# Rotary embedding on one core: the opening store of zeros and batch 0's one-row store are taken out, and the five loads are issued first

## The chip, the cores and the metric

The kernel runs on one core of a Trainium2 chip. The metric is the device time of one execution in microseconds (us). The kernel before took 316.7 us as the median of three runs (316.62 to 316.84). A core has five engines that work side by side, each on its own list of instructions: VectorE (DVE in the profile), ScalarE (ACT), GpSimd (POOL), SyncE (SP) and TensorE, which has no work here. Data between the chip's main memory (HBM) and the core's own memory of 128 partitions moves by DMA. A DMA is issued by an engine and carried out by 16 DMA engines, which serve several queues: here the one that GpSimd fills (q0 in the profile) and the one that SyncE fills (q1).

## The reference

The input `x` has 8 batches of 2048 positions, 16 heads and 64 values each, in float32: 8.39 MB a batch. Each head is rotated by the angles of its position:

```python
def reference(x, cos, sin):                      # cos, sin: 2048 x 32
    x1 = x[..., :head_dim // 2]
    x2 = x[..., head_dim // 2:]
    cos = cos[None, :, None, :]
    sin = sin[None, :, None, :]
    out1 = x1 * cos - x2 * sin
    out2 = x1 * sin + x2 * cos
    return np.concatenate([out1, out2], axis=-1).astype(np.float32)
```

So the whole input is read once and the whole output is written once, with two products and a sum for each value.

## The kernel before, in words

A batch is one tile `xt` of 128 partitions: partition p holds positions 16p to 16p + 15, which the code calls its `J` = 16 rows, of 1024 values each. "One row" below means one of these sixteen on all partitions. The tile is float16 while HBM holds float32, so a load and a store convert on the way; both are issued by GpSimd. There are `NBUF` = 5 tiles, so batches 5, 6 and 7 are loaded into the tiles of batches 0, 1 and 2, and each of these loads waits until the store of that earlier batch has landed.

*Constants.* SyncE issues three loads: `sin` (L40), `head`, which is the first two rows of batch 0 in float32 (L41), and `cos` (L45). ScalarE converts them to float16: `sin_h` with a negated half (L95, L96), the two rows into batch 0's tile (L91), and `cos_h` (L97).

*Rotation.* `rotate` is three VectorE operations on whole rows: the product with `sin_h` into a temporary tile `v` (L73), the product with `cos_h` in place (L79), and the sum (L81). Batch 0 is rotated in two parts: rows 0 and 1, which came by `head`, and then the 14 rows that load 0 brings. The other batches are rotated whole.

*Order on GpSimd's queue.* The code writes out the start of it as `ring`: load 0, the opening store, load 1, the one-row store `first`, then loads 2, 3 and 4. The opening store (L85) writes one float32 zero into the first value of each partition's first row of batch 0's output: 128 values in all. `first` (L107) writes row 0 of batch 0, waits for its rotation, and also waits for the opening store to have landed, since it overwrites the zeros. Then `store` (L60) writes batch 0 from row 1 on (15 rows). The order of the later stores and loads is chosen when the kernel is built, by the planner of the framework, from the waits that each has; GpSimd then takes its instructions in that fixed order, and an instruction that waits holds up all behind it. In the profile the order after load 4 is: stores of batches 0 and 1, loads 5 and 6, stores 2 and 3, load 7, stores 4, 5 and 6.

*The end.* Batch 7 leaves in three parts: rows 0 to 8 (`gate`, L141), rows 9 to 13 (`rest`, L143), and rows 14 and 15, which ScalarE converts back to float32 (L151) and SyncE stores (L152) once `gate` has landed.

Of the kernel before, what the change touches and what calls it, by code (L numbers as in the profile page):

```python
# [1 line left out]

# [4 lines left out]


@with_exitstack  # L10
def kernel(
    ctx: ExitStack,
    tc: tile.TileContext,
    x: bass.AP,
    cos: bass.AP,
    sin: bass.AP,
    out: bass.AP,
):
    nc = tc.nc
    f16 = mybir.dt.float16  # L20
    f32 = mybir.dt.float32

    B, S, H, D = x.shape
    Dh = D // 2
    P = nc.NUM_PARTITIONS
    J = S // P
    NBUF = 5

    const_pool = ctx.enter_context(tc.tile_pool(name="rope_const", bufs=1))
    io_pool = ctx.enter_context(tc.tile_pool(name="rope_io", bufs=NBUF))  # L30
    tmp_pool = ctx.enter_context(tc.tile_pool(name="rope_tmp", bufs=1))

    JA = 2
    head = const_pool.tile([P, JA, H, D], f32)
    x0 = x[0].rearrange("(p j) h d -> p j (h d)", j=J)
    sin_f = const_pool.tile([P, J, Dh], f32)
    cos_f = const_pool.tile([P, J, Dh], f32)
    cos_h = const_pool.tile([P, J, Dh], f16)
    sin_h = const_pool.tile([P, J, D], f16)
    nc.sync.dma_start(out=sin_f, in_=sin.rearrange("(p j) d -> p j d", j=J))  # L40
    nc.sync.dma_start(  # L41
        out=head.rearrange("p j h d -> p (j h d)"),
        in_=x0[:, 0:JA, :].rearrange("p j f -> p (j f)"),
    )
    nc.sync.dma_start(out=cos_f, in_=cos.rearrange("(p j) d -> p j d", j=J))  # L45

    loads = []

    def load(b):
        xt = io_pool.tile([P, J, H, D], f16)  # L50
        j0 = JA if b == 0 else 0
        dma = nc.gpsimd.dma_start(  # L52
            out=xt[:, j0:J, :, :].rearrange("p j h d -> p (j h d)"),
            in_=x[b].rearrange("(p j) h d -> p j (h d)", j=J)[:, j0:J, :].rearrange("p j f -> p (j f)"),
        )
        loads.append(dma)
        return xt

    def store(b, xt, j0=0):
        return nc.gpsimd.dma_start(  # L60
            out=out[b].rearrange("(p j) h d -> p j (h d)", j=J)[:, j0:J, :].rearrange("p j f -> p (j f)"),
            in_=xt[:, j0:J, :, :].rearrange("p j h d -> p (j h d)"),
        )

    def rotate(xt, j0, j1):
        v = tmp_pool.tile([P, J, H, D], f16)
        n = j1 - j0
        js = slice(j0, j1)
        shape = [P, n, H, 2, Dh]
        sin_b = sin_h[:, js, :].rearrange("p j (e d) -> p j e d", e=2).unsqueeze(2).to_broadcast(shape)  # L70
        cos_b = cos_h[:, js, :].unsqueeze(2).to_broadcast([P, n, 2 * H, Dh])
        xe = xt[:, js, :, :].rearrange("p j h (e d) -> p j h e d", e=2)
        nc.vector.tensor_mul(  # L73
            out=v[:, js, :, :].rearrange("p j h (e d) -> p j h e d", e=2),
            in0=xe[:, :, :, ::-1, :],
            in1=sin_b,
        )
        xw = xt[:, js, :, :].rearrange("p j h (e d) -> p j (h e) d", d=Dh)
        nc.vector.tensor_mul(out=xw, in0=xw, in1=cos_b)  # L79
        xa = xt[:, js, :, :].rearrange("p j h d -> p (j h d)")  # L80
        nc.vector.tensor_add(out=xa, in0=xa, in1=v[:, js, :, :].rearrange("p j h d -> p (j h d)"))  # L81


    tiles = [load(0)]
    opening = nc.gpsimd.dma_start(  # L85
        out=out[0].rearrange("(p j) h d -> p j (h d)", j=J)[0:P, 0, 0:1],
        in_=nc.const_aps.tensor(0.0, [P, 1], f32),
        allow_slow_non_contiguous=True,
    )
    tiles.append(load(1))  # L90
    nc.scalar.copy(  # L91
        out=tiles[0][:, 0:JA, :, :].rearrange("p j h d -> p (j h d)"),
        in_=head.rearrange("p j h d -> p (j h d)"),
    )
    nc.scalar.copy(out=sin_h[:, :, Dh:D], in_=sin_f)  # L95
    nc.scalar.mul(out=sin_h[:, :, 0:Dh], in_=sin_f, mul=-1.0)  # L96
    nc.scalar.copy(out=cos_h, in_=cos_f)  # L97
    rotate(tiles[0], 0, JA)
    def part(b, j0, j1):
        return (  # L100
            out[b].rearrange("(p j) h d -> p j (h d)", j=J)[:, j0:j1, :].rearrange("p j f -> p (j f)"),
            tiles[b][:, j0:j1, :, :].rearrange("p j h d -> p (j h d)"),
        )

    def store_rows(b, j0, j1):
        dst, src = part(b, j0, j1)
        return nc.gpsimd.dma_start(out=dst, in_=src)  # L107

    first = store_rows(0, 0, 1)
    tc.add_manual_dep(  # L110
        first.ins,
        opening.ins.name,
        mybir.DependencyInfo(mybir.DependencyClass.Sync, mybir.DependencyReason.DATA),
        reason="the result replaces the zeros",
    )
    ring = [loads[0], opening, loads[1], first]
    for b in range(2, NBUF):
        tiles.append(load(b))
        ring.append(loads[b])
    for a, b in zip(ring[1:], ring[:-1]):  # L120
        tc.add_manual_dep(
            a.ins,
            b.ins.name,
            mybir.DependencyInfo(mybir.DependencyClass.NoSync, mybir.DependencyReason.DATA),
            reason="order of the ring",
        )
    for b in range(B):
        rotate(tiles[b], JA if b == 0 else 0, J)
        if b < B - 1:
            st = store(b, tiles[b], 1 if b == 0 else 0)  # L130
            if b == 0:
                tc.add_manual_dep(
                    st.ins,
                    first.ins.name,
                    mybir.DependencyInfo(mybir.DependencyClass.NoSync, mybir.DependencyReason.DATA),
                    reason="order of the ring",
                )
        if b + NBUF < B:
            tiles.append(load(b + NBUF))
    dst, src = part(B - 1, 0, 9)  # L140
    gate = nc.gpsimd.dma_start(out=dst, in_=src)  # L141
    dst, src = part(B - 1, 9, J - JA)
    rest = nc.gpsimd.dma_start(out=dst, in_=src)  # L143
    tc.add_manual_dep(
        rest.ins,
        gate.ins.name,
        mybir.DependencyInfo(mybir.DependencyClass.NoSync, mybir.DependencyReason.DATA),
        reason="order of the ring",
    )
    dst, src = part(B - 1, J - JA, J)  # L150
    nc.scalar.copy(out=head.rearrange("p j h d -> p (j h d)"), in_=src)  # L151
    end = nc.sync.dma_start(out=dst, in_=head.rearrange("p j h d -> p (j h d)"))  # L152
    tc.add_manual_dep(
        end.ins,
        gate.ins.name,
        mybir.DependencyInfo(mybir.DependencyClass.Sync, mybir.DependencyReason.DATA),
        reason="the last rows go out behind this part",
    )


# [1 line left out]
_INS = ['x', 'cos', 'sin']  # L162
_OUTS = [((8, 2048, 16, 64), 'float32')]


# [23 lines left out]
```

## Time and profile before

| What | Value |
|---|---|
| Median of three runs | 316.7 us (316.62 to 316.84) |
| Span of the profiled execution | 314.8 us |
| VectorE busy | 209.1 us (66% of the span), 27 instructions |
| ScalarE busy | 6.8 us (2%), 6 instructions |
| GpSimd busy | 10.4 us (3%), 23 instructions |
| VectorE, one whole batch, each of three operations | 8.692 us |
| GpSimd, one DMA issue | 0.53 to 0.67 us |
| VectorE's idle time that loads of x ended | 29.8 us, in two waits (4.84 and 24.96) |

The median lies 1.9 us above the profiled span: the span runs from the first to the last instruction of one profiled execution.

The trace gives for each DMA the time of its issue and the time from issue to landing. Their sum is the time at which it landed:

| DMA | Issued, us | To landing, us | Landed, us |
|---|---|---|---|
| load 0 (14 rows) | 1.25 | 22.2 | 23.45 |
| cos | 1.63 | 22.0 | 23.63 |
| opening store | 1.92 | 21.9 | 23.82 |
| load 1 | 2.45 | 40.9 | 43.35 |
| `first` (1 row) | 27.13 | 17.5 | 44.63 |
| load 2 | 27.65 | 36.3 | 63.95 |
| load 4 | 28.71 | 73.8 | 102.51 |
| store 0 (15 rows) | 50.11 | 70.6 | 120.71 |
| store 1 | 76.29 | 63.8 | 140.09 |
| load 5 | 121.29 | 38.0 | 159.29 |
| load 6 | 140.34 | 38.3 | 178.64 |
| store 2 | 140.86 | 57.1 | 197.96 |
| load 7 | 198.29 | 38.3 | 236.59 |
| store 4 | 198.82 | 57.1 | 255.92 |
| store 6 | 211.99 | 82.6 | 294.59 |
| `gate` (9 rows) | 263.09 | 42.4 | 305.49 |
| `rest` (5 rows) | 263.62 | 47.9 | 311.52 |
| rows 14 and 15, by SyncE | 305.55 | 8.4 | 313.95 |

How to read it: a DMA that is issued early waits in the queue behind the earlier ones, so the time to landing is mostly waiting. The difference of two neighbours' landings is the time that the later one had the DMA engines for. The trace also has a record of every packet that a DMA engine moved, with its start, length and size; a whole batch is 128 packets, one for each partition, eight on each of the 16 engines.

### The profile page before, as it was taken

To read this page: it belongs to the slowest core of one execution; us is meant where nothing else is said; L and a number is where in the kernel's file an instruction comes from. 1 tells how busy PE (TensorE), PEld (TensorE's weight loads), DVE (VectorE), ACT (ScalarE), POOL (GpSimd) and SP (SyncE) were. 2 spreads that over 40 slices of the span, in tenths; PEclk is the share of its full clock that TensorE was granted. 3 is DMA by queue.
4 is the path that set the end of the run, shared out by engine and by line. 5 is a ranking of instruction groups with operands and counts; after the bars stand their busy time and mean duration, and the time that the engine had idled before them with its cause. 6 is when DMAs were issued, how large, how long until landed. Compare 5 with 4: busy or idle time off the path is not lost.

```text
span 314.8 us, 125 instructions
## 1 busy us (share of the span) xinstructions
DVE 209.1 (66%) x27; ACT 6.8 (2%) x6; POOL 10.4 (3%) x23
## 2 busy tenths in 40 slices
DVE  0108999999999999999679999980009993000000
ACT  3200000000000000000000000000000002000000
POOL 2002000000000000010000000200000001000000
DMA  9899999999999899999999999999999999999998
GB/s 283 187 262 200 200 266 200 200 262 204 200 200 325 375 500 400 400 333 266 200 200 212 387 400 400 475 458 266 200 300 433 400 400 525 408 400 400 433 427 339
DMA packets 3201, 101.71 MB, mean 323 GB/s; under 512 B 385, under 2 KB 385, under 8 KB 769
## 3 DMA queue, kind: packets, MB, share of 16 engines
q0 software_dynamic: 2624, 99.09, 98.1%
q1 hardware_dynamic: 576, 2.62, 2.2%
q14 instruction: 1, 0.00, 0.0%
HBM read 67.63 MB, written 67.11 MB: 428 GB/s over the span
## 4 chain that ended last, share of the span: by engine, by line
DVE 25%; another core or an unknown queue 20%; DMA 19%; issue 18%; ACT 1%; POOL 1%; SPq 0%; POOLq 0%; DVEq 0%; ACTq 0%
DMA xt<-in_x_dram 12%; DVE xt L81 8%; DVE xt L79 8%; DVE v L73 8%; DMA cos_f<-in_cos_dram 7%; ACT head L151 1%; POOL out_dram L60 0%; POOL xt L52 0%; ACT cos_h L97 0%; SPq L41 0%; SPq L40 0%; POOLq L52 0%; DVEq L73 0%; ACTq L151 0%
## 5 line engine op out<-in xcount | busy, mean ns | idle before, releaser
L73 DVE TENSOR_TENSOR v<-xt,sin_h 128x16384 f16<-128x16384 f16 (+2 forms) x9 | 69.7, 7744 | 40.0 <-DMA xt<-in_x_dram 29.8
L79 DVE TENSOR_TENSOR xt<-xt,cos_h 128x16384 f16<-128x16384 f16 (+2 forms) x9 | 69.7, 7744 | 13.4 <-ACT cos_h L97 13.1
L81 DVE TENSOR_TENSOR xt<-xt,v 128x16384 f16<-128x16384 f16 (+2 forms) x9 | 69.7, 7744 | 0.3
L52 POOL DMA_DIRECT2D xt<-in_x_dram x8 | 4.4, 557 | 120.2 <-DMA out_dram<-xt 119.4
L151 ACT CAST head<-xt 128x2048 f32<-128x2048 f16 x1 | 1.9, 1897 | 238.6 <-DVE xt L81 238.6
L60 POOL DMA_DIRECT2D out_dram<-xt x7 | 3.7, 535 | 58.6 <-DVE xt L81 58.6
L141 POOL DMA_DIRECT2D out_dram<-xt x1 | 0.5, 533 | 50.6 <-DVE xt L81 50.6
L91 ACT CAST xt<-head 128x2048 f16<-128x2048 f32 x1 | 1.9, 1897 | 3.4 <-DMA head<-in_x_dram 3.4
L107 POOL DMA_DIRECT2D out_dram<-xt x1 | 0.5, 531 | 24.1 <-DVE xt L81 24.1
L95 ACT ACT_TABLE_LOAD x1 | 1.3, 1283 | 0.7 <-PEq L173 0.7
L97 ACT CAST cos_h<-cos_f 128x512 f16<-128x512 f32 x1 | 0.6, 617 | 13.7 <-DMA cos_f<-in_cos_dram 13.7
L95 ACT CAST sin_h<-sin_f 128x512 f16<-128x512 f32 x1 | 0.6, 617 | 1.5 <-DMA sin_f<-in_sin_dram 1.5
L96 ACT ACTIVATE sin_h<-sin_f 128x512 f16<-128x512 f32 x1 | 0.6, 624 | 0.0
L85 POOL DMA_DIRECT2D out_dram<-const-float32-0.0 x1 | 0.5, 545 | 0.0
L143 POOL DMA_DIRECT2D out_dram<-xt x1 | 0.5, 533 | 0.0
L173 POOL MEMSET const-float32-0.0<- 128x1 f32 x1 | 0.1, 98 | 0.2 <-issue 0.2
L173 POOL MEMSET const-bfloat16-1.0<- 128x1 bf16 x1 | 0.1, 101 | 0.0
L173 POOL MEMSET const-float32-1.0<- 128x1 f32 x1 | 0.1, 98 | 0.0
L173 POOL MEMSET const-uint8-127<- 128x1 uint8 x1 | 0.1, 98 | 0.0
## 6 DMA issues: line engine op xcount, KB each, us to landing
xt<-in_x_dram POOLq DMA_DIRECT2D x7, 4096.0 KB, 38.3
out_dram<-xt POOLq DMA_DIRECT2D x1, 7680.0 KB, 70.6
out_dram<-xt POOLq DMA_DIRECT2D x1, 4608.0 KB, 42.4
xt<-in_x_dram POOLq DMA_DIRECT2D x1, 3584.0 KB, 22.2
out_dram<-xt POOLq DMA_DIRECT2D x1, 2560.0 KB, 47.9
head<-in_x_dram SPq DMA_DIRECT2D x1, 1024.0 KB, 6.9
out_dram<-head SPq DMA_DIRECT2D x1, 1024.0 KB, 8.4
out_dram<-xt POOLq DMA_DIRECT2D x1, 512.0 KB, 17.5
```

What stands on the lines that cost most here:

```text
L52: dma = nc.gpsimd.dma_start(out=xt[:, j0:J, :, :].rearrange("p j h d -> p (j h d)"), in_=x[b].rearrange("(p j) h d -> p j (h d)", j=J)[:, ...
L60: return nc.gpsimd.dma_start(out=out[b].rearrange("(p j) h d -> p j (h d)", j=J)[:, j0:J, :].rearrange("p j f -> p (j f)"), in_=xt[:, j0:J ...
L73: nc.vector.tensor_mul(out=v[:, js, :, :].rearrange("p j h (e d) -> p j h e d", e=2), in0=xe[:, :, :, ::-1, :], in1=sin_b,)
L79: nc.vector.tensor_mul(out=xw, in0=xw, in1=cos_b)
L81: nc.vector.tensor_add(out=xa, in0=xa, in1=v[:, js, :, :].rearrange("p j h d -> p (j h d)"))
L85: opening = nc.gpsimd.dma_start(out=out[0].rearrange("(p j) h d -> p j (h d)", j=J)[0:P, 0, 0:1], in_=nc.const_aps.tensor(0.0, [P, 1], f32 ...
L91: nc.scalar.copy(out=tiles[0][:, 0:JA, :, :].rearrange("p j h d -> p (j h d)"), in_=head.rearrange("p j h d -> p (j h d)"),)
L95: nc.scalar.copy(out=sin_h[:, :, Dh:D], in_=sin_f)
L96: nc.scalar.mul(out=sin_h[:, :, 0:Dh], in_=sin_f, mul=-1.0)
L97: nc.scalar.copy(out=cos_h, in_=cos_f)
L107: return nc.gpsimd.dma_start(out=dst, in_=src)
L151: nc.scalar.copy(out=head.rearrange("p j h d -> p (j h d)"), in_=src)
```

## The change

The opening store goes, with its place in `ring` and the dependency of `first` on it. `first` goes with its helper `store_rows`, and batch 0's store writes all 16 rows. `ring` then holds the five loads alone, so GpSimd issues them without a store between them.

```diff
     tiles = [load(0)]
-    opening = nc.gpsimd.dma_start(
-        out=out[0].rearrange("(p j) h d -> p j (h d)", j=J)[0:P, 0, 0:1],
-        in_=nc.const_aps.tensor(0.0, [P, 1], f32),
-        allow_slow_non_contiguous=True,
-    )
     tiles.append(load(1))
...
-    def store_rows(b, j0, j1):
-        dst, src = part(b, j0, j1)
-        return nc.gpsimd.dma_start(out=dst, in_=src)
-
-    first = store_rows(0, 0, 1)
-    tc.add_manual_dep(
-        first.ins,
-        opening.ins.name,
-        mybir.DependencyInfo(mybir.DependencyClass.Sync, mybir.DependencyReason.DATA),
-        reason="the result replaces the zeros",
-    )
-    ring = [loads[0], opening, loads[1], first]
+    ring = [loads[0], loads[1]]
     for b in range(2, NBUF):
...
         if b < B - 1:
-            st = store(b, tiles[b], 1 if b == 0 else 0)
-            if b == 0:
-                tc.add_manual_dep(
-                    st.ins,
-                    first.ins.name,
-                    mybir.DependencyInfo(mybir.DependencyClass.NoSync, mybir.DependencyReason.DATA),
-                    reason="order of the ring",
-                )
+            store(b, tiles[b])
```

## The prediction

> **What bounds the kernel now.** I read the page's slices and queues first, because a kernel that moves eight batches in and out and does three vector operations on each can only be bound by one of these two.
>
> ```profile
> DVE  0108999999999999999679999980009993000000
> ...
> DMA  9899999999999899999999999999999999999998
> ...
> q0 software_dynamic: 2624, 99.09, 98.1%
> q1 hardware_dynamic: 576, 2.62, 2.2%
> ...
> HBM read 67.63 MB, written 67.11 MB: 428 GB/s over the span
> ```
>
> The vector engine (DVE) has holes; the DMA row has none. GpSimd's queue (q0) and SyncE's (q1) together fill the 16 DMA engines for 98.1% + 2.2% of the span. So the end is set by how much time the transfers need, plus any moment in which the engines have nothing queued. Next I read the timeline of GpSimd (POOL), which says when each transfer enters the queue, with the two places where DVE waits for data.
>
> ```profile
> 1.25 0.67 POOL L52 DMA_DIRECT2D xt<-in_x_dram  x1 [0.81 <-PEq L184]
> ...
> 1.92 0.55 POOL L85 DMA_DIRECT2D out_dram<-const-float32-0.0  x1
> 2.45 0.54 POOL L52 DMA_DIRECT2D xt<-in_x_dram  x1
> ...
> 27.13 0.53 POOL L107 DMA_DIRECT2D out_dram<-xt  x1 [24.14 <-DVE xt L81]
> 27.65 1.60 POOL L52 DMA_DIRECT2D xt<-in_x_dram  x3
> ...
> 50.11 0.54 POOL L60 DMA_DIRECT2D out_dram<-xt  x1 [20.85 <-DVE xt L81]
> ...
> 76.29 0.54 POOL L60 DMA_DIRECT2D out_dram<-xt  x1 [25.64 <-DVE xt L81]
> ...
> 121.29 0.53 POOL L52 DMA_DIRECT2D xt<-in_x_dram  x1 [44.47 <-DMA out_dram<-xt]
> ...
> 140.34 0.53 POOL L52 DMA_DIRECT2D xt<-in_x_dram  x1 [18.51 <-DMA out_dram<-xt]
> 140.86 1.06 POOL L60 DMA_DIRECT2D out_dram<-xt  x2
> ...
> 159.38 8.69 DVE L73 TENSOR_TENSOR v<-xt,sin_h 128x16384 f16<-128x16384 f16 x1 [4.84 <-DMA xt<-in_x_dram]
> ...
> 198.29 0.53 POOL L52 DMA_DIRECT2D xt<-in_x_dram  x1 [56.37 <-DMA out_dram<-xt]
> ```
>
> Columns: start in us, length, engine, line, operation, and in brackets the idle time before it with what ended it. With each transfer's time to landing (the table of landings above) this gives the queue's order: transfers land in the order in which they were issued, one behind the other. From the landing of batch 0's store (120.71) to that of batch 6's (294.59) nine whole batches pass: 173.88 / 9 = **19.32 us for a batch**, a load and a store alike. A transfer is always issued long before its turn: batch 0's store enters at 50.11, while loads are due until 102.51. Issue times therefore have slack of tens of us, and only what the queue carries counts.
>
> **What the change removes, part by part.**
>
> *The opening store* (128 values of 4 bytes, one for each partition). Its issue, 0.55 us on POOL, is in front of load 1 only, which then enters at 1.92 instead of 2.45; load 0 is moving until 23.45, which hides that. In the queue it is an item between load 0 and load 1. It landed 0.37 us behind load 0 (23.82 against 23.45); part of that is the way of its completion, as the packet records give its data 15 ns on each engine. Cost between 0 and 0.37; I take 0.05, since the 15 ns are its own row.
>
> *The one-row store* `first`. One row of sixteen is worth 19.32 / 16 = 1.21 us by the rate. It landed 44.63 - 43.35 = 1.28 behind load 1. There is a third row: from load 0's landing to load 2's, 63.95 - 23.45 = 40.50 us pass, and two loads are worth 38.64, so 1.86 us go to all that is small there: opening, `first`, the last packet of `cos` (it rides between load 0 and load 1), and something more. The packet records show the something: the last packet of load 1 took 2.70 to 2.89 us on fifteen of the 16 engines, where such a packet takes 2.43 everywhere else. It is the packet ahead of `first`. So `first` costs between 1.28 and 1.86; by the records 1.24 (spacing of the packets) + 0.33 (the slowed packet) = 1.57, which I take.
>
> *Batch 0's store* grows from 15 rows to 16: 120.71 - 102.51 = 18.20 now, 19.32 then: +1.12.
>
> *Issues.* POOL loses two of them, 0.55 + 0.53 us, and the wait of 24.14 us for the first rotation; loads 2 to 4 go in at about 2.5 to 4.1 us instead of 27.65 to 29.25. Nothing waits for them sooner: load 1 keeps the engines until 43. The number of transfers in the queue at once becomes five at the start; in the trace five whole ones stand there too, from 211.99 (batch 3's store, load 7, batches 4, 5 and 6), and the issue then took 0.53 as ever. So I cost the early issue at nothing; if the queue did hold POOL up, it would do so with a full queue, and behind it on POOL stands only batch 0's store, which has about 50 us of cover.
>
> *The wait that lengthens: `cos`.*
>
> ```profile
> 1.63 22.05 DMA cos_f<-in_cos_dram
> ...
> 23.70 0.63 ACT cos_h L97
> ```
>
> This is the chain of waits near the start. `cos` (256 KB on SyncE's queue) needs 22 us because its packets take turns with load 0's, one against one; its completion is a packet of its own, which now gets its turn while the opening's tiny packet stands on the other side. Without the opening, load 1's first packet stands there: 19.32 / 8 = 2.42 us (a batch is 128 rows, eight for each engine). I expect `cos` to land at about 26.1 instead of 23.7 and with it DVE's first products and every DVE operation up to batch 4 to be 2.4 us late. What is late next: batch 0's store is issued at about 52.5, with its turn at about 101, so 48 us of cover; batch 1's at 78.7, turn at about 120. The delay ends at batch 5, where DVE waits 4.84 us for load 5 anyway and would then wait 2.4. Cost on the end: nothing.
>
> **The sum**: -0.05 (opening) - 1.57 (`first`) + 1.12 (the sixteenth row) = -0.50 us. From both sides: -0 - 1.28 + 1.12 = -0.16 and, all small things together, -1.86 + 1.12 = -0.74. The slowed packet need not vanish: if it belongs to the first change from loading to storing, it moves to load 4, and the saving is 0.50 - 0.33 = 0.17. Between these I take 0.4, nearer to the records. The profiled execution's span goes from 314.8 to 314.4. The median of the runs is 1.9 above that span, which lies around it and isn't touched: 316.7 - 0.4 = **316.3 us**.
>
> The Trainium skill speaks of each transfer's fixed cost (DMA: Bandwidth & Descriptors, Anatomy of one DMA): about 2.0 us on top of the bytes. By that the two transfers removed would be worth 4.0 us. The row against it: the last but one store (five rows) landed 6.0 us behind the nine rows ahead of it, and 5/16 of 19.32 is 6.04, so behind a full queue no fixed cost shows.
>
> **The rivals.**
> - *Each transfer costs its setup.* Speaking for it: the 1.86 us above, more than the bytes of one row. Against: the five-row store, and 19.32 for nine batches in a row, each a transfer. Its size from rows: a load on an empty queue, load 0, lands 22.2 us after issue; its 14 rows are 16.9 and sin, cos and head (1.5 MB at that rate) 3.6, so 1.7 us of setup; two of them are 3.4: 316.7 - 3.4 - 0.2 = 313.1. The skill's figure would give 312.5.
> - *Nothing is saved*: the slowed packet goes with the first real store wherever it stands, and the extra 0.58 between the landings of loads 0 and 1 (19.90 for a load) is `cos`. Then 0.1 to 0.2 remain: 316.6.
> - *A dry queue (slower).* POOL takes its instructions in a written order, which the build's planner chooses; now it is stores 0 and 1, loads 5 and 6, stores 2 and 3, load 7, stores 4 to 6. With two instructions fewer ahead, the planner could put load 5 ahead of store 1. Load 5 waits for store 0 to land; store 1, ready at 76, would be stuck behind it, and at 120.7 the engines would stand still. Price: 0.55 from landing to the load's issue, plus 1.7 of setup as for load 0 (2.2 by sin: 2.8 to landing, 0.6 of it bytes), so 2.3 to 2.8 each. In that order it happens at stores 0, 1 and 2, so about 7.5 us: 323.8. It decides as soon as one load of the second round precedes a store that could cover it. Against it: store 1 is ready 44 us before store 0 lands, and that isn't close. A flip the other way (store 2 ahead of load 5) costs nothing, as the queue stays full.
> - *`cos` reaches the end (slower).* 2.4 us late all the way: 316.3 + 2.4 = 318.7. It decides from a delay of 4.84 us, at batch 5; even then the last store is issued at 263.09 for a turn at 294.59. Against it, then, both margins.
>
> **How the numbers follow.** Forecast 0.65, setup 0.03, nothing saved 0.14, dry queue 0.12, `cos` to the end 0.06. What a measurement of this kernel can tell from no change is about 0.2%, 0.63 us. The forecast's own range, 0.16 to 0.74 saved and 0.2 for the spread of runs (316.62 to 316.84), is 315.8 to 316.7; a third of its chance lies beyond 0.63 saved. Faster: 0.03 + 0.22 = 0.25. Slower: 0.12 + 0.06 = 0.18. Same: 0.57. For the range I leave out setup, the dry queue and the far half of the `cos` case: 315.6 to 317.4.
>
> **What would show it.** In the profile after: five loads issued by about 4.1 us; `cos` landing at about 26 us and DVE's second operation at about 26.8; the landings of loads 1 to 4 19.3 apart, load 2 landing at about 62.3; store 0 landing 19.3 behind load 4, at about 120.3; DVE's wait before batch 5 down from 4.84 to about 2; the end of everything 0.4 earlier; POOL's order as now. A packet of 2.7 us or more ahead of store 0 would show that the slowing belongs to the first store. I'd be wrong if the DMA row had a hole, if load 5 were issued before store 1, or if a batch took other than 19.3 us while loads follow loads.

## The result and the profile after

The changed kernel takes 317.3 us (median of 20 runs, 316.99 to 317.63) against 316.67 for the kernel before (20 runs beside it): a ratio of 1.002, 95% interval 1.0015 to 1.0026. It is slower by 0.63 us, 0.2% of the time, where 0.4 us faster was forecast. The profiled span went from 314.8 to 315.5 us.

The page of the changed kernel, its queues and HBM:

```profile
span 315.5 us, 121 instructions
...
DMA  9899999999999999999999999999999999999998
...
q0 software_dynamic: 2448, 99.09, 98.0%
q1 hardware_dynamic: 576, 2.62, 2.2%
HBM read 67.63 MB, written 67.11 MB: 427 GB/s over the span
```

The bytes are the same and the DMA row still has no hole at this resolution, so the lost time isn't a queue that ran dry. Its timeline (start, length, engine, line, operation, idle time before with what ended it):

```profile
1.25 2.79 POOL L52 DMA_DIRECT2D xt<-in_x_dram  x5 [0.80 <-PEq L161]
...
54.94 0.54 POOL L60 DMA_DIRECT2D out_dram<-xt  x1 [50.91 <-DVE xt L81]
...
81.12 0.54 POOL L60 DMA_DIRECT2D out_dram<-xt  x1 [25.64 <-DVE xt L81]
...
121.72 0.53 POOL L52 DMA_DIRECT2D xt<-in_x_dram  x1 [40.06 <-DMA out_dram<-xt]
...
141.31 0.53 POOL L52 DMA_DIRECT2D xt<-in_x_dram  x1 [19.06 <-DMA out_dram<-xt]
141.83 1.06 POOL L60 DMA_DIRECT2D out_dram<-xt  x2
...
160.09 8.69 DVE L73 TENSOR_TENSOR v<-xt,sin_h 128x16384 f16<-128x16384 f16 x1 [0.72 <-DMA xt<-in_x_dram]
```

The five loads go in at once and the order on GpSimd is the same as before. The answers for the DMAs issued at 2.95 (load 3), 3.47 (load 4) and 54.94 (store 0), with the time to landing as the last number, say where the loss arises:

```profile
xt<-in_x_dram POOLq DMA_DIRECT2D x1, 4096.0 KB, 78.7
...
xt<-in_x_dram POOLq DMA_DIRECT2D x1, 4096.0 KB, 98.6
...
out_dram<-xt POOLq DMA_DIRECT2D x1, 66.5
```

They landed at 81.7, 102.1 and 121.4. In the kernel before, loads 3 and 4 were issued at 28.18 and 28.70:

```profile
xt<-in_x_dram POOLq DMA_DIRECT2D x1, 4096.0 KB, 55.0
...
xt<-in_x_dram POOLq DMA_DIRECT2D x1, 4096.0 KB, 73.8
```

So there load 4 landed 19.3 us behind load 3. Store 0's landing is now 0.7 us later than the 120.7 of before, which is the whole loss. Load 4 had the engines for 20.4 us and store 0 for 19.3; a batch takes 19.32. The packet records name the place: on all 16 engines the last packet of load 4, the one ahead of the first store, took 3.1 to 3.7 us instead of 2.43, on the mean **1.03 us** too long. In the kernel before, the same happened at the last packet of load 1, ahead of `first`, with 0.35 us. No later change from loading to storing shows it, in either kernel.

By the starts of the packets, from load 1 to store 1: the new slow packets cost +1.03, the old ones are gone, -0.35, and 16 rows in place of `first` and 15 rows give -0.04. That is +0.64 of the 0.72 us between the spans.

### The profile page after: what moved, and what is told of

Its sections match the earlier page's. It is cut to its first block, busy times and chain, and to the rows that moved or that the text cites. A ratio compares the mean times of both kernels' runs of the same rounds, so it can differ in the third digit from the quotient of the medians.

```text
span 315.5 us, 121 instructions
## 1 busy us (share of the span) xinstructions
DVE 209.1 (66%) x27; ACT 6.8 (2%) x6; POOL 9.3 (3%) x21
## 4 chain that ended last, share of the span: by engine, by line
DVE 25%; DMA 21%; another core or an unknown queue 18%; issue 18%; POOL 1%; ACT 1%; SPq 0%; POOLq 0%; DVEq 0%; ACTq 0%
DMA xt<-in_x_dram 12%; DMA cos_f<-in_cos_dram 9%; DVE xt L81 8%; DVE xt L79 8%; DVE v L73 8%; ACT head L128 1%; POOL out_dram L60 1%; POOL xt L52 0%; ACT cos_h L92 0%; SPq L41 0%; SPq L40 0%; POOLq L60 0%; DVEq L73 0%; ACTq L128 0%
```

## The experiments

The question is why the slow packets cost 0.35 us ahead of the one-row store and 1.03 ahead of the whole one. Each timed experiment has its ratio against the kernel before, run on the same chip. "Slow packets" are the us by which the packets of a transfer are longer than usual, as a mean over the 16 engines, each with the transfer in which they stand. They come from the packet records of one profiled execution of each kernel. The medians are over 8 to 20 executions, except where it says one run, and over three for the kernel before:

```
kernel                       early              in load 4    median us
before                       0.35 (load 1)      0            316.7
after                        0                  1.03         317.3
no opening                   0.33 (load 1)      0            316.68
no one-row store             0                  1.38         317.48
opening into batch 7         0                  0.79         317.34
opening on SyncE             0                  1.02         317.43
one row behind load 4        0                  0.64         317.44
store 0 behind load 2        1.28 (load 2)      0            317.55
two rows behind load 1       1.03 (load 1)      0            317.37
one head behind load 1       0                  1.18         317.28
half a row behind load 1     0.05 (load 1)      0.65         316.79
copy inside the core         1.23 (load 1)      0            319.93, one run
copy from HBM to HBM         0                  0.98         319.62, one run
rows by SyncE's queue        0.22 (load 1)      0.24         320.42, one run
two halves together, once    0.63 (load 2)      1.16         316.92
two halves together, again   0.26 (load 1)      0            316.82
two halves apart             0.03 (load 1)      0.18         316.43
three halves apart           0.07 (load 1)      0            316.50
```

The slow packets reach the end nearly one for one. Add up all that is too long in the packets of the first five loads, and the time of the same profiled execution goes with the sum: 0.2 to 0.3 us of it and 316.4 to 316.5 us (two and three halves apart), 0.35 to 0.4 and 316.6 (before, no opening, two halves again), 0.74 and 316.92 (half a row), 1.1 to 1.5 and 317.2 to 317.7 (the eight others that move the same bytes). The first execution of the two halves together alone stands outside, at 1.96 and 318.92.

**The opening store alone left out.**

```diff
-    opening = nc.gpsimd.dma_start(...)
...
-    ring = [loads[0], opening, loads[1], first]
+    ring = [loads[0], loads[1], first]
```

> The opening store alone is left out; the one-row store and the order of the loads stay. The result showed that the last packets ahead of the first real store of the queue are slow: 0.33 us over the usual 2.43 in the kernel before, 1.01 us over it in the changed kernel. Theory A (the opening pays beforehand what the first store costs): the slow packets ahead of the one-row store grow from about 0.33 to about 1.0 us over, and the time is about 0.6 us above before, like the changed kernel's 317.3. Theory B (the cost goes by the size of the first real store, or by what is queued ahead of it, and the opening does nothing but let cos land earlier): the slow packets stay at 0.33 us over, and the time is within 0.1 us of before.

Ratio 0.9997 (0.9988 to 1.0006), slow packets 0.33: theory A fails. No effect of the opening on the time can be seen (the interval is -0.4 to +0.2 us). What it did was to let `cos` land early: ScalarE's conversion, which waits for it, starts at 28.29 here and at 23.70 with the opening.

**The one-row store alone left out.**

```diff
-    first = store_rows(0, 0, 1)
...
-    ring = [loads[0], opening, loads[1], first]
+    ring = [loads[0], opening, loads[1]]
...
-            st = store(b, tiles[b], 1 if b == 0 else 0)
+            store(b, tiles[b])
```

> The opening store stays, the one-row store alone is left out, so that batch 0 leaves as one store and the five loads go first with the opening between loads 0 and 1. Theory A (the opening pays beforehand): the last packets of load 4 are at most 0.33 us over 2.43, the time is 0.3 to 0.5 us below before (about 316.2). Theory B (size of the first store, or what is queued ahead of it): the last packets of load 4 are about 1.0 us over, and the time is 0.6 us above before.

Ratio 1.0026 (1.0016 to 1.0035), slow packets 1.38 in load 4. The whole loss of the change comes with this part of it.

**An opening elsewhere, and on another queue.**

The first diff is against the changed kernel, the second against the first:

```diff
     tiles = [load(0)]
+    opening = nc.gpsimd.dma_start(
+        out=out[B - 1].rearrange("(p j) h d -> p j (h d)", j=J)[0:P, 0, 0:1],
+        in_=nc.const_aps.tensor(0.0, [P, 1], f32),
...
-    ring = [loads[0], loads[1]]
+    ring = [loads[0], opening, loads[1]]
```

```diff
-    opening = nc.gpsimd.dma_start(
-        out=out[B - 1].rearrange("(p j) h d -> p j (h d)", j=J)[0:P, 0, 0:1],
+    opening = nc.sync.dma_start(
+        out=out[0].rearrange("(p j) h d -> p j (h d)", j=J)[0:P, 0, 0:1],
...
-    ring = [loads[0], opening, loads[1]]
+    ring = [loads[0], loads[1]]
```

> The changed kernel with an opening store again, but into the first values of batch 7's output instead of batch 0's. If the cost belongs to the addresses that are written first (the opening must touch the same part of the output), the last packets of load 4 stay 1.0 us over and the time stays 0.6 above before. If it belongs to the queue or to the DMA engines (any store opens them), they are at most 0.33 over and the time is 0.3 to 0.5 below before.

> The changed kernel with the opening store again, to batch 0's output, but issued by SyncE on its own queue behind cos. If the cost belongs to GpSimd's queue, the last packets of load 4 stay 1.0 us over and the time is 0.6 above before. If it belongs to the DMA engines or to the addresses, they are at most 0.33 over and the time is 0.2 to 0.5 below before.

Ratios 1.0020 (1.0010 to 1.0029) and 1.0026 (1.0015 to 1.0036); load 4 is slow by 0.79 and 1.02. A store of 4 bytes a partition takes nothing off the cost that these runs could show, wherever it goes. The 0.79 came with about 0.4 us of slightly long packets spread over loads 1 to 4 of that execution.

**Size or place?** The one-row store moved behind load 4 (against the kernel without the opening):

```diff
-    first = store_rows(0, 0, 1)
-    ring = [loads[0], loads[1], first]
+    ring = [loads[0], loads[1]]
     for b in range(2, NBUF):
         tiles.append(load(b))
         ring.append(loads[b])
+    first = store_rows(0, 0, 1)
+    ring.append(first)
```

And the whole store moved ahead of load 3 (against the changed kernel):

```diff
+    rotate(tiles[0], JA, J)
     for b in range(2, NBUF):
+        if b == 3:
+            ring.append(store(0, tiles[0]))
         tiles.append(load(b))
...
```

The later loop then leaves batch 0 out.

> Five loads first, no opening, and then the one-row store, now behind load 4, with the other 15 rows behind it. So far: the opening changes nothing (without it the slow packets ahead of the one-row store were 0.34 us over the usual 2.43; with it and without the one-row store, those of load 4 were 1.35 over). Theory B1 (the cost of the first large transfer out goes by the size of its packets: 4 KB for one row, 64 KB for a whole batch): the last packets of load 4 are about 0.3 over, nothing more between the one-row store and the 15 rows, and the time is that of before (316.6 to 316.8). Theory B2 (it goes by what is ahead: five loads in a row instead of two): they are about 1.0 over, and the time is 317.3 to 317.6.

> No opening and no one-row store; batch 0 leaves as one store, but ahead of loads 3 and 4 instead of behind them. Theory B1 (size of the packets): the last packets of load 2, ahead of that store, are 1.0 to 1.4 us over 2.43, as those of load 4 are in the changed kernel; time 317.3 to 317.5. Theory B2 (number of loads ahead): with three loads ahead they are about 0.5 over (between the 0.33 for two and the 1.0 to 1.3 for five); time about 316.9. Under both, the queue is never empty, although the order of the later loads and stores differs from the changed kernel.

The whole store costs 1.28 with three loads ahead as with five (ratio 1.0031, 1.0011 to 1.0051), so the number of loads ahead isn't it. The one row right ahead of the other 15 costs 0.64, between the two theories, and the time is that of the changed kernel (ratio 1.0023, 1.0011 to 1.0035). The profiled execution also had 0.57 us of long packets within loads 2 and 3, which bring the sum to 1.28; why they are there stays open.

**The early store's size.** Two rows, one head (64 values) and half a row instead of one row, behind load 1, with no opening. `row0` and `src0` are batch 0's output and tile with all 16 rows of a partition in one line; the later store of batch 0 begins where the early one ends. In this order:

```diff
-    first = store_rows(0, 0, 1)
+    first = store_rows(0, 0, JA)
```

```diff
-    first = store_rows(0, 0, 1)
+    first = nc.gpsimd.dma_start(out=row0[:, 0:D], in_=src0[:, 0:D])
```

```diff
-    first = store_rows(0, 0, 1)
+    first = nc.gpsimd.dma_start(out=row0[:, 0:8 * D], in_=src0[:, 0:8 * D])
```

> The early store behind load 1 takes two rows (packets of 8 KB) instead of one, batch 0's other store 14; no opening. Theory B1 (size): the last packets of load 1 are over by a little more than with one row, 0.35 to 0.45 us. Theory B2 (what is ahead): 0.28 to 0.34, as with one row. Time within 0.2 us of before under both.

> The early store behind load 1 takes one head of row 0 alone (64 values, packets of 256 bytes out), the other store of batch 0 everything else; no opening. Theory B1 (size): the last packets of load 1 are less than 0.3 us over, near 0, and either the first large store (behind load 4) then pays 1.0 after all, as it did behind the opening store of 4 bytes (time 317.4), or nothing is left to pay and the time is 0.2 to 0.3 below before. Theory B2: as with one row, 0.3 over, nothing behind load 4, time as before.

> The early store behind load 1 takes half of row 0 (8 heads, packets of 2 KB out), the other store of batch 0 everything else; no opening. So far, over the usual 2.43 us: packets of 256 bytes cost nothing early and left 1.18 behind load 4; 4 KB cost 0.33 early and left nothing; 8 KB cost 1.03 early and left nothing. Theory B1 (size): about 0.15 to 0.2 early, nothing behind load 4, time 0.1 to 0.2 us below before. Rival (there is a least size that settles it, between 256 bytes and 4 KB): nothing or little early, and 1.0 to 1.4 behind load 4, time 317.3.

Two rows pay the full 1.03 early and leave nothing (ratio 1.0014, 1.0004 to 1.0025); neither expectation had more than 0.45 there. One head pays nothing and leaves 1.18 (1.0014, 1.0005 to 1.0023). Half a row came out as neither of its two expectations, and is the telling one: it pays 0.05 and takes part of the rest away, 0.65 is left (1.0005, 0.9995 to 1.0014). So an early store of half a row or one row doesn't merely move the cost, it lowers it: 0.70 and 0.33 in all against 1.03.

**What is it that comes first?** Three transfers that belong to no result, added to the changed kernel: `head` copied inside the core's own memory, rows 0 and 1 of batch 0 copied from HBM to HBM, and `head` stored to HBM by SyncE.

In this order (`last` is the tile of load 4, taken before that load is issued):

```diff
+    early = nc.gpsimd.dma_start(
+        out=last[:, 0:JA, :, :].rearrange("p j h d -> p (j h d)"),
+        in_=head.rearrange("p j h d -> p (j h d)"),
+    )
+    ring.append(early)
...
```

```diff
+    early = nc.gpsimd.dma_start(
+        out=out[0].rearrange("(p j) h d -> p j (h d)", j=J)[:, 0:JA, :].rearrange("p j f -> p (j f)"),
+        in_=x0[:, 0:JA, :].rearrange("p j f -> p (j f)"),
+    )
+    ring = [loads[0], loads[1], early]
...
```

```diff
+    early = nc.sync.dma_start(
+        out=out[0].rearrange("(p j) h d -> p j (h d)", j=J)[:, 0:JA, :].rearrange("p j f -> p (j f)"),
+        in_=head.rearrange("p j h d -> p (j h d)"),
+    )
```

> The changed kernel with an extra copy behind load 1 on GpSimd's queue, from the core's memory to the core's memory: head (two rows in float32, 8 KB a partition) into the tile that load 4 overwrites later; it is no part of the result. If the one-time cost comes from the first large read of the core's memory by the DMA engines, load 1's or load 2's packets beside the copy are slow (about 1 us) and load 4's last packets are not. If it comes from the first large write to HBM, load 4's last packets stay 1.0 to 1.4 us over.

> The changed kernel with an extra copy behind load 1 on GpSimd's queue, from HBM to HBM: rows 0 and 1 of batch 0's input into its output, which its store overwrites later; it is no part of the result. If the one-time cost comes from the first large write to HBM, the cost (about 1 us) shows around the copy and load 4's last packets are not slow. If it comes from the first large read of the core's memory, load 4's last packets stay 1.0 to 1.4 us over.

> The changed kernel with an extra store on SyncE's queue, behind cos: head (two rows of input in float32, packets of 8 KB, no conversion) into batch 0's first rows of output, which its store overwrites later; it is no part of the result. If the one-time cost belongs to GpSimd's queue, load 4's last packets stay 1.0 to 1.4 us over; if it belongs to the DMA engines or to memory, they are not slow, and packets early on are.

With the copy inside the core, the DMAs issued at 8.34 (the copy), 8.86 (load 2), 46.98 (load 4) and 52.48 (store 0):

```profile
last<-head POOLq DMA_DIRECT2D x1, 512.0 KB, 38.4
...
xt<-in_x_dram POOLq DMA_DIRECT2D x1, 4096.0 KB, 57.2
...
last<-in_x_dram POOLq DMA_DIRECT2D x1, 4096.0 KB, 57.7
...
out_dram<-xt POOLq DMA_DIRECT2D x1, 71.6
```

From load 2's landing (66.1) to load 4's (104.7) pass 38.6 us, two batches, and store 0 follows 19.4 later: load 4 has nothing left to pay, the 1.23 stood in load 1, ahead of the copy. With the copy from HBM to HBM, the DMAs issued at 2.95, 3.48 and 3.99 (loads 2, 3, 4):

```profile
xt<-in_x_dram POOLq DMA_DIRECT2D x1, 4096.0 KB, 61.9
...
xt<-in_x_dram POOLq DMA_DIRECT2D x1, 4096.0 KB, 80.7
...
xt<-in_x_dram POOLq DMA_DIRECT2D x1, 4096.0 KB, 100.4
```

Load 3 lands 19.3 behind load 2, load 4 20.2 behind load 3: the cost is still there, 0.98 by the packets, although 1 MB had been written to HBM, into the very rows that store 0 then writes. So it comes with the first large reads of the **core's own memory** by the DMA engines, which until the first store have only written it. SyncE's store, whose packets take turns with those of load 1 from 25 us on, leaves 0.24 late and has 0.22 at load 1's end, besides some long packets within loads 0 and 1: reads on the other queue count too, so it isn't GpSimd's queue.

The copy inside the core and SyncE's store speak against two more rivals. Both read `head` early, not batch 0's tile, and yet the first read of that tile lost all or most of its cost, so the cost doesn't go with the address that is read. And it isn't the conversion: the copy converts from float32 to float16 as the loads do, and SyncE's store converts nothing. Each of the three kernels ran once, so the sizes are those of one execution; their times say nothing, as they move up to 1 MB more each way.

**Amount read or size of the packets?** Row 0 as two halves together, the halves apart (behind loads 1 and 2), and a third half behind load 3:

The diffs, in this order, are against the kernel with half a row, again against it, and against the second:

```diff
+    second = nc.gpsimd.dma_start(out=row0[:, 8 * D:H * D], in_=src0[:, 8 * D:H * D])
-    ring = [loads[0], loads[1], first]
+    ring = [loads[0], loads[1], first, second]
```

```diff
         ring.append(loads[b])
+        if b == 2:
+            second = nc.gpsimd.dma_start(out=row0[:, 8 * D:H * D], in_=src0[:, 8 * D:H * D])
+            ring.append(second)
```

```diff
-        if b == 2:
-            second = nc.gpsimd.dma_start(out=row0[:, 8 * D:H * D], in_=src0[:, 8 * D:H * D])
+        if b in (2, 3):
+            f = slice((b - 1) * 8 * D, b * 8 * D)
+            second = nc.gpsimd.dma_start(out=row0[:, f], in_=src0[:, f])
             ring.append(second)
```

> Row 0 leaves behind load 1 as two stores of half a row (packets of 2 KB), one right behind the other; the other 15 rows behind load 4; no opening. What is known by now: a copy from the core's memory to itself behind load 1 pays the one-time cost (1.23 us) and frees load 4's last packets of it, a copy from HBM to HBM does not, so the cost comes with the first large reads of the core's memory. One row (2 KB read from each partition) paid 0.33 and left nothing, half a row paid 0.05 and left 0.65. If it goes by the amount that has been read: 0.33 early in all and nothing left, time as before. If it goes by the size of the packets: 0.05 to 0.1 early and 0.3 to 0.65 left behind load 4, time 0.1 above before.

> The same two half rows, the first behind load 1, the second behind load 2. If each early read takes its part of the cost while little waits behind it: 0.05 behind load 1, 0.05 to 0.3 behind load 2, nothing behind load 4, time 0.05 to 0.25 below before (the best version so far). If it goes by the size of the packets: 0.3 to 0.65 left behind load 4, time 0.1 to 0.2 above before.

> A third half row (the first half of row 1) leaves early, behind load 3, on top of those behind loads 1 and 2; batch 0's last store has 14.5 rows. With one half row 0.65 was left behind load 4, with two apart 0.18. If the cost left goes by the amount read before: 0 to 0.1 left, slow packets 0.1 to 0.15 in all, time 0.3 to 0.4 us below before. If the spread does not go on working: 0.18 left as with two, and time as with two less nothing (0.2 to 0.3 below before).

> The same kernel as with the two half rows together, once more, since its profiled execution took 318.9 us while its median was 316.9, so that its packets tell nothing. By amount read: 0.2 to 0.35 early in all and at most 0.2 left behind load 4. By size of packets: at most 0.1 early and 0.3 to 0.65 left.

The two halves together ran twice, and the two traces disagree. In the repetition they behave as one row does: 0.26 early, nothing left (ratio 1.0003, 0.9994 to 1.0012). In the first run (0.9986, 0.9956 to 1.0016) the profiled execution took 318.92 us against a median of 316.92. There `cos` came late, and the halves entered the queue only as load 1 was ending:

```profile
38.57 0.62 ACT L92 CAST cos_h<-cos_f 128x512 f16<-128x512 f32 x1 [17.54 <-DMA cos_f<-in_cos_dram]
...
41.99 0.54 POOL L106 DMA_DIRECT2D out_dram<-xt  x1 [39.54 <-DVE xt L81]
42.52 0.54 POOL L107 DMA_DIRECT2D out_dram<-xt  x1
43.05 1.60 POOL L52 DMA_DIRECT2D xt<-in_x_dram  x3
```

The engines stood idle for 0.6 us on the mean ahead of the halves, the first packets of load 2 were 0.63 us too long, and the last packets of load 4 were 1.16 us too long, although a whole row had been read by then. So the amount read does not decide it alone. The repetition, with nothing left ahead of store 0, speaks for the amount read and against the size of the packets; the medians can't tell the two theories apart, as these lay 0.1 us from each other. What the 22 executions do show is that a late cost of 1.16 is not the rule, since by the relation below the table that would put the median near 317.4.

Apart, the halves cost 0.21 in all (0.18 of it behind load 4, where nothing was expected to be left), three of them 0.07, in one execution each: reads that come in small portions with a load behind each seem to get the cost down further. The two halves apart are faster than the kernel before, by a little: 0.9989 (0.9981 to 0.9998). With three, the interval reaches 1 (0.9993, 0.9984 to 1.0002); 0.3 to 0.4 us faster was expected of it, and 0.2 was measured.

## Why the prediction was wrong

- **The bound** was right: the DMA engines are busy throughout, 19.32 us for a batch in both kernels by the packets' starts. From store 0's landing on the two run alike, 0.7 us apart (load 7 goes in at 198.99 against 198.29).
- **The slowed packet** is the step that failed. The prediction saw it, priced it at 0.33 and took it as part of what `first` costs; for the case that it belongs to the first change from loading to storing it let the same 0.33 move to load 4 and still save 0.17. It does belong there, and its size doesn't go with it: it is 1.03 in the changed kernel, 0.8 to 1.4 in all kernels whose first large read of the core's memory is a whole batch. The lower bound of the saving was therefore no bound: its 0.33 was measured in a kernel where `first` kept the cost small. `first` took 1.57 us for a row worth 1.21, and in return the whole store behind it did not pay 1.03, a price that the trace of before never shows. The sum had no term for slow packets ahead of store 0; with 1.03 there in place of nothing, the forecast's -0.50 becomes +0.53; 0.63 was measured. The sign named for this, a packet of 2.7 us or more ahead of store 0, did come: 3.1 to 3.7 us.
- **The range**: 317.3 lies inside the stated 315.6 to 317.4, and that is luck. Its upper part was left for a late `cos`, which cost nothing here.
- **The opening at 0.05**: nothing speaks against it; left out alone, the time stays (0.9997), but the interval is too wide to tell 0.05 from nothing.
- **The sixteenth row**: +1.12 forecast, 1.21 by the packets' starts (18.11 to 19.32).
- **`cos`**: the direction was right, and with one packet of load 1 in between, ScalarE's conversion of `cos` starts at 26.1 to 26.2 us, as in the kernels with half a row, with halves apart and with store 0 behind load 2. In the changed kernel it lands later:

```profile
1.64 26.87 DMA cos_f<-in_cos_dram
...
28.54 0.63 ACT cos_h L92
```

  Load 0's first packet (at 5.24) got ahead of the last packet of `head` on one engine (7.56), and everything on SyncE's queue there slipped by one more packet of load 0. DVE's wait before batch 5 shrank to 0.72 us, not to 2; it was still a wait, and the delay ended there as forecast.
- **The early issue and POOL's order**: as forecast, no cost, order unchanged. The dry queue and the rival in which `cos` reaches the end did not come in the changed kernel; nor did the setup of each transfer, whose 3.4 us the result excludes. The slower side came from a mechanism that had no place in the list except as a smaller gain.

The prediction also held that the early issue of loads 2 to 4 gains nothing. That is so as long as `cos` comes in time. In the long execution of the two halves together it didn't, and loads 2 to 4, behind the early store, entered only from 43.05 on; in the changed kernel they don't wait for `cos` and are in the queue by about 4 us.

What in the DMA engines makes the first reads slow is open. The runs show what brings it and what lowers it in most executions, not the part of the chip in which it sits, nor why one execution paid it again after a row had been read.

## What to carry to other kernels

When a trace shows an irregular cost next to a piece that is to be removed, ask whether the piece causes it or keeps it small; the trace with the piece in place can't tell, and the cost read there is no bound for the time without. In a kernel that loads for a long time before it first stores, try to let a small part of the result leave between the loads (here half a row to one row, 2 to 4 KB of float32 a partition), and look at the last packets ahead of the first large store; the gain here was 0.2% of the time. The loads behind such a store wait for its rotation, so it has to be ready well before the queue runs empty. And before giving a queue's irregular packet to a transfer, compare it with the later places of the same kind: in the trace of before no later change from loading to storing showed it, which pointed to a cost of the first reads.

## What the runs showed of the hardware

- Ahead of the first large read of the core's memory by the DMA engines, the last load packet on each of the 16 engines was too long, by 0.8 to 1.4 us on the mean, in the nine kernels where that read is a whole batch (or all of it but one head), two rows or a copy of `head`; later stores there didn't show it.
- Early reads, in one execution each: 128 bytes from each partition neither paid nor lowered it; 1 KB left 0.65; 2 KB in one store paid 0.33 and left nothing (0.35 in the kernel before); 4 KB paid 1.03 and left nothing. But in one of two executions 2 KB read early as two stores left 1.16. Writing 1 MB to HBM before left 0.98.
- Packets of two queues take turns one by one on each engine, and a transfer's completion takes a turn of its own: `cos`, 256 KB, whose packets take 0.1 us each, reached ScalarE at 23.7, 26.1 or 28.5 us behind packets of 2.1 to 2.4 us. Where more of `head` came behind load 0's packets on an engine, it was later still: 31.0 and 38.6 us in the two executions of the halves together.
